# Attention with a shared bias on one core: the emission order from a list scheduler that models the queues, q/k transposes in halves, bias blocks four to a slot, first loads in quarters

## The chip, the cores and the metric

The kernel runs on one core of one Trainium2 chip. The metric is the device time of one execution in microseconds; lower is better. Times quoted at a place ("at 13.03") are counted from the start of the profiled span. In the views, PE is TensorE (PEld its weight load), ACT is ScalarE, DVE is VectorE, POOL is GpSimd, and SP only issues transfers here.

## What is computed

Softmax attention with one additive bias that all batches and heads share. There are 4 x 8 = 32 heads, 1024 queries and keys, and a head dimension of 64:

```python
batch, n_heads, seq_len, head_dim = 4, 8, 1024, 64
scores = (1.0 / np.sqrt(head_dim)) * np.matmul(q, k.transpose(0, 1, 3, 2))
scores = scores + bias                      # bias: (1, 1, 1024, 1024)
scores_max = np.max(scores, axis=-1, keepdims=True)
attn = np.exp(scores - scores_max) / (np.sum(np.exp(scores - scores_max), axis=-1, keepdims=True) + 1e-8)
return np.matmul(attn, v)
```

The kernel leaves the maximum out and uses exp(s + b) = exp(s) x exp(b). The row sums come out of the last matmul, because a column of ones stands behind v.

## The kernel before

**Units of work.** Two heads form a pair, so there are 16 pairs. q and k of a pair are transposed on PE (`L90`) into `px`. DVE copies k out as `kT`, with both heads stacked on the 128 partitions (`L101`), and q as `qT`, once for each head with the other head's half masked to zero (`L96`). A *bank* is a block of scores of 128 keys by 512 queries of one head: one matmul of 128x512 (`L126`) into one of three PSUM banks of a tile `ps`. There are 512 banks, 32 in a pair (2 halves of the queries, 8 key chunks, 2 heads).

**A slot** is one tile `ps`: up to three banks are filled on PE and taken by one exponential on ACT, which writes `E` in bf16 (`L128`). Two `ps` tiles alternate, so that the fill of one slot waits until ACT has emptied the slot two before it. The bias goes through the same two tiles: blocks of it are transposed on PE into `pb` (`L134`), and ACT takes the exponential into `eb` (`L138`). The bias is thus transformed once, in six slots of 3, 3 and 2 blocks for each half of the queries.

**Behind ACT.** DVE multiplies two banks of `E` at a time by `eb` (`L143`, 256 times). Then PE multiplies each bank by v: four matmuls of 128x65 (`L155`), which sum over the eight key chunks in a tile `po`. A finished `po` (one head, half of the queries) is divided by its row sums on DVE (`rs` in `L165`, `oall` in `L166`), and SP writes out each head.

**PSUM banks.** Six of the eight belong to the two `ps` tiles. The other two are called `xa` and `xb`. `po` of the pair's first head always takes `xa` and that of the second head `xb`. `px`, from the third pair on, always takes `xa`: 16 transposes of q, or 16 of k, at once.

**What sets the order.** Every engine runs its instructions in the order of the program, which is written out by hand under a manual schedule. A loop goes over the slots. After each slot's fill and exponential it emits up to three or four banks of the product with v (those whose multiplication was emitted at least `LAG = 3` steps ago), then one multiplication, the divisions that are due, and two more multiplications. A transposition is emitted at fixed counts of the products with v:

```python
pend_t += [(pr, 0, (pr - 2) * 32 + 8), (pr, 1, (pr - 2) * 32 + 24)]
```

**Start.** The first halves of k and q of pair 0 come as fp32 in one transfer each on SP and ACT (`k0f`, `q0f`), are cast, transposed and copied by the function `first`; all other loads go through POOL's queue. Eight matmuls on zeros (`wm`) run on PE while the first loads are under way. Slot 0 holds one bank, all others three, the last one.

Of the kernel before, what the change touches and what calls it, by code (L numbers as in the profile page):

```python
# [15 lines left out]
def kernel(  # L16
# [44 lines left out]
    mask = consts.tile([P, 2, S], BF)  # L61
# [3 lines left out]
    q0f = consts.tile([P, 2, QC, D], F32)  # L65
# [16 lines left out]
    def transpose(pr, which):  # L82
        transpose_pe(pr, which)()

    def transpose_pe(pr, which):
        src = raws[pr][which]
        px = ps_x.tile([P, NCH, P], BF, tag="xb" if pr < 2 and which else "xa", name="px")
        for c in range(NCH):
            for t in range(2):
                nc.tensor.transpose(px[t * D:(t + 1) * D, c, :], src[:, t, c, :], ident[:])  # L90

        def copy():
            if which == 0:

                dst = kvp.tile([P, 2, NCH * P], BF, name="qT")
                nc.vector.tensor_tensor(  # L96
                    dst[:], px.rearrange("p c q -> p (c q)").unsqueeze(1).to_broadcast([P, 2, NCH * P]),
                    mask[:], op=ALU.mult)
            else:
                dst = kvp.tile([P, NCH, P], BF, name="kT")  # L100
                nc.vector.tensor_copy(dst[:], px[:])  # L101
            trs[(pr, which)] = dst
        return copy
# [4 lines left out]
    slots = [list(range(1))] + [list(range(i, min(i + 3, NB))) for i in range(1, NB, 3)]  # L108
# [4 lines left out]
    def e_at(b, n):  # L113
        b = b + 2
# [4 lines left out]
    def s_slot(g):  # L119
        ps = ps_s.tile([P, 3, HQ], F32, tag="s", name="ps")  # L120
        sl = slots[g]
        n = len(sl)
        for j, b in enumerate(sl):
            pr, h, qh, kc = banks[b]
            qT, kT = trs[(pr, 0)], trs[(pr, 1)]
            nc.tensor.matmul(ps[:, j, :], kT[:, kc, :], qT[:, h, qh * HQ:(qh + 1) * HQ],  # L126
                             start=True, stop=True)
        nc.scalar.activation(e_at(sl[0], n), ps[:, :n, :], ACTF.Exp, scale=scale)  # L128

    def b_slot(qh, kcs):  # L130
        ps = ps_s.tile([P, 3, 2 * HQ], BF, tag="s", name="pb")
        for j, kc in enumerate(kcs):
            for i in range(QC):
                nc.tensor.transpose(ps[:, j, i * P:(i + 1) * P],  # L134
                                    btraw[:, qh * QC + i, :].rearrange("p (kp kc) -> p kc kp", kc=NCH)[:, kc, :],
                                    ident[:])
        n = len(kcs)
        nc.scalar.activation(eb[:, qh, kcs[0]:kcs[0] + n, :], ps[:, :n, :HQ], ACTF.Exp)  # L138

    def mul_pair(b, n=2):  # L140
        pr, h, qh, kc = banks[b]
        e = e_at(b, n)
        nc.vector.tensor_tensor(e, e, eb[:, qh, kc:kc + 1, :].to_broadcast([P, n, HQ]), op=ALU.mult)  # L143
# [4 lines left out]
    def av_bank(b):  # L148
# [23 lines left out]

    av_order = []
    for u in range(0, NB, 16):
        av_order += [u + 2 * i for i in range(8)] + [u + 2 * i + 1 for i in range(8)]

    with tc.manual_schedule():

        nc.sync.dma_start(out=k0f.rearrange("p t c d -> p t (c d)"), in_=kf[0][:, :, :QC * D])
        nc.scalar.dma_start(out=q0f.rearrange("p t c d -> p t (c d)"), in_=qf[0][:, :, :QC * D])  # L180
# [6 lines left out]
        raws[0] = (qr0, kr0)  # L187
        nc.gpsimd.dma_start(out=kr0[:, :, QC:, :].rearrange("p t c d -> p t (c d)"), in_=kf[0][:, :, QC * D:])
        nc.gpsimd.dma_start(out=qr0[:, :, QC:, :].rearrange("p t c d -> p t (c d)"), in_=qf[0][:, :, QC * D:])
        nc.gpsimd.dma_start(out=btraw[:, :QC, :], in_=bf_[:, :QC, :])  # L190
        for t in range(2):
            for u in range(2):
                nc.vector.memset(mask[t * D:(t + 1) * D, u, :], 1.0 if t == u else 0.0)  # L193
# [11 lines left out]
        nc.scalar.copy(kr0[:, :, :QC, :], k0f[:])  # L205
        nc.vector.tensor_copy(qr0[:, :, :QC, :], q0f[:])  # L206
        kT0 = kvp.tile([P, NCH, P], BF, name="kT")
        qT0 = kvp.tile([P, 2, NCH * P], BF, name="qT")
        trs[(0, 0)], trs[(0, 1)] = qT0, kT0
        def first(half):  # L210
            cs = slice(half * QC, (half + 1) * QC)
            pk = ps_x.tile([P, QC, P], BF, tag="xb", name="pk")
            pq = ps_x.tile([P, QC, P], BF, tag="xa", name="pq")
            for px, which in ((pk, 1), (pq, 0)):
                for c in range(QC):
                    for t in range(2):
                        nc.tensor.transpose(px[t * D:(t + 1) * D, c, :], raws[0][which][:, t, half * QC + c, :], ident[:])  # L217
            if half == 0:
                nc.scalar.copy(kT0[:, cs, :], pk[:])
            else:  # L220
                nc.vector.tensor_copy(kT0[:, cs, :], pk[:])  # L221
            qs = slice(half * HQ, (half + 1) * HQ)
            nc.vector.tensor_tensor(qT0[:, :, qs],  # L223
                                    pq.rearrange("p c q -> p (c q)").unsqueeze(1).to_broadcast([P, 2, HQ]),
                                    mask[:, :, qs], op=ALU.mult)
        first(0)
        s_slot(0)

        order = [("S", g) for g in range(1, NS)]
        halves = [(0, 1, 2), (3, 4, 5), (6, 7)]  # L230
        for at, x in ((5, (0, halves[0])), (7, (0, halves[1])), (9, (0, halves[2])),
                      (11, (1, halves[0])), (13, (1, halves[1])), (15, (1, halves[2]))):
            order.insert(at, ("B",) + x)

        mul_done = {}
        eb_have = set()
        mul_next = 0
        exp_b = 1
        av_next = 0

        pend_t = []
        for pr in range(2, NP):
            pend_t += [(pr, 0, (pr - 2) * 32 + 8), (pr, 1, (pr - 2) * 32 + 24)]
        LAG = 3

        def muls(n):
            nonlocal mul_next
            while n and mul_next < NB:
                pr, h, qh, kc = banks[mul_next]
                w = 2  # L250
                if mul_next + w > exp_b or (qh, kc) not in eb_have:
                    break
                mul_pair(mul_next, w)
                for b in range(mul_next, mul_next + w):
                    mul_done[b] = step
                mul_next += w
                n -= 1

        t_wait = None
        for step, item in enumerate(order):  # L260
            if item[0] == "S":
                g = item[1]
                s_slot(g)
                new_b = slots[g][-1] + 1
            else:
                b_slot(item[1], item[2])
                new_b = exp_b
            late = []
            if step == 1:
                first(1)  # L270
            if step == 8:
                transpose(1, 1)
                transpose(1, 0)
                load_qk(3)
            quota = 4 if (exp_b - av_next) > 18 else 3
            if t_wait is not None and step >= t_wait:
                pr, which, _ = pend_t.pop(0)
                late.append(transpose_pe(pr, which))
                t_wait = None
                quota = 1  # L280
                if which == 1:
                    if pr + 2 < NP:
                        load_qk(pr + 2)
                    load_v(pr)
            while quota and av_next < NB:
                b = av_order[av_next]
                if mul_done.get(b, 10 ** 9) > step - LAG:
                    break
                e = av_bank(b)
                if e:  # L290
                    late.append(e)
                av_next += 1
                quota -= 1
                if pend_t and av_next == pend_t[0][2]:
                    t_wait = step + 2

            muls(1)
            for f in late:
                f()
            muls(2)  # L300
            exp_b = new_b
            if item[0] == "B":
                for kc in item[2]:
                    eb_have.add((item[1], kc))

        while av_next < NB:
            muls(1)
            b = av_order[av_next]
            while mul_next <= b:
                muls(1)  # L310
            e = av_bank(b)
            if e:
                e()
            av_next += 1
# [30 lines left out]
```

## Time and profile before

| | us |
|---|---|
| median of 3 runs | 262.85 (262.81 to 264.83) |
| the profiled execution | 265.01 |
| its span in the trace | 263.1 |
| busy: ACT, DVE, PE | 242.0, 227.2, 220.6 |

The granted TensorE clock was 0.998 over the span. The span leaves out some 1.9 us that the profiled execution's own time holds around it. An engine's busy time counts the overlap of two of its instructions once. In a timeline a row merges equal instructions that follow each other: its start, how long it lasts in all, and in brackets the idle time ahead of it with what ended it.

### The profile page before, as it was taken

Reading aid. Unit: us, or ns where it says so; the run is one execution under the profiler, and the core shown is the slowest. Engines: PE = TensorE matmul, PEld = TensorE weight load, DVE = VectorE, ACT = ScalarE, POOL = GpSimd, SP = SyncE. Lnnn points to the kernel's source line nnn. Section 1 sums busy time; section 2 is a strip of 40 time slices with the busy share of each in tenths; the row PEclk is TensorE's granted clock in tenths of the full one; section 3 lists DMA queues with packets and bytes.
Section 4 is the critical chain, followed back from the end, with each engine's and each line's share of the span. In section 5 each row is a group of like instructions: output and inputs, shape, how many; then the busy total and the mean of one; then the engine's idle time right before and its main releaser. Section 6 shows DMA issues by size and latency. Waiting matters only on the chain.

```text
span 263.1 us, 7177 instructions
## 1 busy us (share of the span) xinstructions
PE 220.6 (84%) x3092; PEld 138.6 (53%) x3144; DVE 227.2 (86%) x425; ACT 242.0 (92%) x182; POOL 52.7 (20%) x72
## 2 busy tenths in 40 slices
PE   7857889888889888898988888888988889898882
PEld 2335655555555555555555555555655555555552
DVE  5218889999899999989989989998999999899893
ACT  4598999999999999999999999999999999999990
POOL 5834004040220404040030404022180000000000
PEclk9999999999999999999999999999999999999999
DMA  7999907759190856729191855819199202011112
GB/s 140 181 217 187 157 0 123 82 97 104 44 159 25 139 40 123 83 67 135 42 156 38 135 36 103 101 45 156 44 160 83 80 2 80 5 40 42 40 44 80
DMA packets 47455, 23.79 MB, mean 90 GB/s; under 512 B 34368, under 2 KB 43072, under 8 KB 47168
## 3 DMA queue, kind: packets, MB, share of 16 engines
q0 software_dynamic: 42272, 14.42, 51.1%
q1 hardware_dynamic: 4880, 8.65, 9.1%
q8 instruction: 24, 0.39, 0.6%
q10 hardware_dynamic: 272, 0.26, 0.4%
q14 instruction: 7, 0.06, 0.1%
HBM read 29.36 MB, written 8.39 MB: 143 GB/s over the span
## 4 chain that ended last, share of the span: by engine, by line
DVE 32%; PE 32%; ACT 31%; issue 3%; ACTq 0%; DVEq 0%
ACT E L128 30%; PE ps L126 21%; DVE E L143 18%; PE po L155 9%; DVE qT L96 6%; DVE kT L101 4%; DVE oall L166 2%; ACT eb L138 2%; DVE mask L193 1%; PE pq L217 1%; DVE rs L165 1%; ACTq L128 0%; DVE qT L223 0%; DVE qr L206 0%; PE px L90 0%
## 5 line engine op out<-in xcount | busy, mean ns | idle before, releaser
L128 ACT ACTIVATE E<-ps 128x1536 bf16<-128x1536 f32 (+1 forms) x172 | 232.7, 1470 | 10.6 <-PE ps L126 7.2
L143 DVE TENSOR_TENSOR E<-E,eb 128x1024 bf16<-128x1024 bf16 x256 | 166.9, 687 | 21.9 <-ACT E L128 11.1
L126 PE MATMUL ps<-qT,kT 128*128 128x512 bf16 x460 | 135.4, 383 | 15.8 <-ACT E L128 10.6
L155 PEld LDWEIGHTS <-E 128*128 128x128 bf16 x2048 | 84.0, 98 | 56.2 <-issue 21.2
L155 PE MATMUL po<-vall,E 128*128 128x65 bf16 x2048 | 93.6, 194 | 17.8 <-DVE qT L96 12.3
L126 PEld LDWEIGHTS <-kT 128*128 128x128 bf16 x512 | 44.4, 98 | 43.6 <-issue 19.1
L74 POOL DMA_DIRECT2D kr<-in_k_dram x15 | 10.5, 702 | 139.9 <-PE px L90 80.8
L166 DVE TENSOR_TENSOR oall<-po,rs 128x256 f32<-128x256 f32 x64 | 27.2, 425 | 2.2
L80 POOL DMA_DIRECT2D vall<-in_v_dram x32 | 28.1, 884 | 2.5 <-DVE qr L206 2.5
L96 DVE TENSOR_TENSOR qT<-px,mask 128x2048 bf16<-128x2048 bf16 x15 | 18.3, 1218 | 0.0
L165 DVE RECIPROCAL rs<-po 128x4 f32<-128x4 f32 x64 | 11.3, 176 | 0.7 <-PE po L155 0.7
L101 DVE COPY kT<-px 128x1024 bf16<-128x1024 bf16 x15 | 10.3, 684 | 0.9 <-PE px L90 0.9
L75 POOL DMA_DIRECT2D qr<-in_q_dram x15 | 10.8, 723 | 0.7 <-DMA vall<-in_v_dram 0.4
L90 PEld LDWEIGHTS <-kr 128*64 128x64 bf16 x240 | 7.1, 109 | 6.4 <-issue 6.4
L90 PE MATMUL px<-ident,qr 128*64 128x128 bf16 x240 | 9.5, 222 | 0.7
L90 PEld LDWEIGHTS <-qr 128*64 128x64 bf16 x240 | 7.2, 109 | 5.6 <-issue 3.4
L90 PE MATMUL px<-ident,kr 128*64 128x128 bf16 x240 | 9.6, 222 | 0.6
L138 ACT ACTIVATE eb<-pb 128x1536 bf16<-128x1536 bf16 (+1 forms) x6 | 8.0, 1332 | 0.0
L134 PEld LDWEIGHTS <-btraw 128*128 128x128 bf16 x64 | 4.8, 147 | 3.2 <-issue 2.5
L134 PE MATMUL pb<-ident,btraw 128*128 128x128 bf16 x64 | 5.0, 226 | 1.8 <-ACT eb L138 1.2
L203 PE MATMUL wm<-zeros 128*128 128x512 bf16 x8 | 3.6, 631 | 1.2 <-DVE zeros L182 1.2
L221 DVE COPY kT<-pk 128x512 bf16<-128x512 bf16 x1 | 0.4, 424 | 3.8 <-PE pk L217 3.8
(25 smaller groups left out, 17.0 us busy)
## 6 DMA issues: line engine op xcount, KB each, us to landing
out_dram<-oall SPq DMA_DIRECT2D x32, 256.0 KB, 2.2
vall<-in_v_dram POOLq DMA_DIRECT2D x32, 128.0 KB, 6.7
kr<-in_k_dram POOLq DMA_DIRECT2D x15, 256.0 KB, 4.0
qr<-in_q_dram POOLq DMA_DIRECT2D x15, 256.0 KB, 5.6
btraw<-in_bias_dram POOLq DMA_DIRECT2D x2, 1024.0 KB, 10.7
q0f<-in_q_dram ACTq DMA_DIRECT2D x1, 256.0 KB, 4.2
k0f<-in_k_dram SPq DMA_DIRECT2D x1, 256.0 KB, 3.7
kr<-in_k_dram POOLq DMA_DIRECT2D x1, 128.0 KB, 4.2
```

Source lines behind the costliest of these rows:

```text
L75: nc.gpsimd.dma_start(out=qr.rearrange("p t c d -> p t (c d)"), in_=qf[pr])
L80: nc.gpsimd.dma_start(out=vall[:, 2 * pr + t, :, :D], in_=vf[pr, :, t])
L90: nc.tensor.transpose(px[t * D:(t + 1) * D, c, :], src[:, t, c, :], ident[:])
L96: nc.vector.tensor_tensor(dst[:], px.rearrange("p c q -> p (c q)").unsqueeze(1).to_broadcast([P, 2, NCH * P]), mask[:], op=ALU.mult)
L101: nc.vector.tensor_copy(dst[:], px[:])
L126: nc.tensor.matmul(ps[:, j, :], kT[:, kc, :], qT[:, h, qh * HQ:(qh + 1) * HQ], start=True, stop=True)
L128: nc.scalar.activation(e_at(sl[0], n), ps[:, :n, :], ACTF.Exp, scale=scale)
L138: nc.scalar.activation(eb[:, qh, kcs[0]:kcs[0] + n, :], ps[:, :n, :HQ], ACTF.Exp)
L143: nc.vector.tensor_tensor(e, e, eb[:, qh, kc:kc + 1, :].to_broadcast([P, n, HQ]), op=ALU.mult)
L155: nc.tensor.matmul(acc[:, i, :], e[:, 0, i * P:(i + 1) * P], vall[:, 2 * pr + h, kc, :], start=(kc == 0 and i == 0), stop=(kc == NCH - 1), ...
L165: nc.vector.reciprocal(rs[:], acc[:, :, D:D1])
L166: nc.vector.tensor_tensor(oall[:, qh * QC:(qh + 1) * QC, :], acc[:, :, :D], rs[:].to_broadcast([P, QC, D]), op=ALU.mult)
```

## The change

1. **Order.** The loop with its quotas and its lag is gone. The program now steps through a model of ACT, PE and DVE with a cost for each operation, and emits on PE and DVE what the model would start next. A fill goes first when it can start; another piece of PE work is put ahead of it only if it would end 100 ns before ACT is through with the slot in between, less the fill's cost.
2. **Transposes.** q and k of a pair are transposed in halves of 8 transposes, each copied by a DVE instruction of half the size. They take whichever of `xa` and `xb` is free, as do the `po` tiles.
3. **Bias.** Four blocks to a slot, so four slots instead of six.
4. **First loads.** k of pair 0 in two pieces on SP, q head by head on ACT and SP; each piece has a cast, transposes and a copy of its own. Slots begin with one and two banks; the last holds two. The masking of the first q halves is replaced by two memsets of zeros.
5. **Last unit.** The products with v of the last 16 banks alternate between the two heads.

The core of the diff:

```diff
-        px = ps_x.tile([P, NCH, P], BF, tag="xb" if pr < 2 and which else "xa", name="px")
-        for c in range(NCH):
+        px = ps_x.tile([P, QC, P], BF, tag=tag, name="px")
+        for c in range(QC):
             for t in range(2):
-                nc.tensor.transpose(px[t * D:(t + 1) * D, c, :], src[:, t, c, :], ident[:])
+                nc.tensor.transpose(px[t * D:(t + 1) * D, c, :], src[:, t, half * QC + c, :], ident[:])
...
-    slots = [list(range(1))] + [list(range(i, min(i + 3, NB))) for i in range(1, NB, 3)]
+    slots = [[0], [1, 2]] + [list(range(i, min(i + 3, NB))) for i in range(3, NB, 3)]
...
-        nc.scalar.activation(eb[:, qh, kcs[0]:kcs[0] + n, :], ps[:, :n, :HQ], ACTF.Exp)
+    def b_exp(qh, k0):
+        nc.scalar.activation(eb[:, qh, k0:k0 + 4, :], open_ps.pop(("B", qh, k0))[:, :4, :], ACTF.Exp)
...
-            po[h] = ps_x.tile([P, QC, D1], F32, tag="xa" if h == 0 else "xb", name="po")
+            po[h] = ps_x.tile([P, QC, D1], F32, tag=tag, name="po")
...
-        nc.sync.dma_start(out=k0f.rearrange("p t c d -> p t (c d)"), in_=kf[0][:, :, :QC * D])
-        nc.scalar.dma_start(out=q0f.rearrange("p t c d -> p t (c d)"), in_=qf[0][:, :, :QC * D])
+        nc.sync.dma_start(out=k0f[:, :, :2].rearrange("p t c d -> p t (c d)"), in_=kf[0][:, :, :2 * D])
+        nc.scalar.dma_start(out=q0f[0].rearrange("p c d -> p (c d)"), in_=qf[0][:, 0, :QC * D])
+        nc.sync.dma_start(out=q0f[1].rearrange("p c d -> p (c d)"), in_=qf[0][:, 1, :QC * D])
+        nc.sync.dma_start(out=k0f[:, :, 2:].rearrange("p t c d -> p t (c d)"), in_=kf[0][:, :, 2 * D:QC * D])
...
-        first(0)
-        s_slot(0)
...
+        def k_first(c0, cast, copy):
+            cs = slice(c0, c0 + 2)
+            cast(kr0[:, :, cs, :], k0f[:, :, cs, :])
+            px = ps_x.tile([P, 2, P], BF, tag="xb", name="px")
...
+            copy(kT0[:, cs, :], px[:])
...
+        k_first(0, nc.scalar.copy, nc.scalar.copy)
+        q_first(0, nc.vector.tensor_copy)
+        s_fill(0)
+        s_exp(0)
+        q_first(1, nc.vector.tensor_copy)
+        s_fill(1)
+        s_exp(1)
+        k_first(2, nc.vector.tensor_copy, nc.vector.tensor_copy)
...
+        EXP, EXP0, QK, AV, TP = 427, 45, 216, 170, 350
+        MUL, COPYQ, COPYK, EVAC, SEM = 600, 650, 420, 620, 80
...
+        for at, x in ((5, (0, 0)), (7, (0, 4)), (11, (1, 0)), (13, (1, 4))):
+            order.insert(at, ("B",) + x)
...
+            limit = 1e12
+            if f:
+                limit = max(f[0], act_end_of(i - 1) - f[1] - 100)
...
+            for c in (pe_piece(), pe_av()):
+                if c is None:
+                    continue
+                start = max(t_pe, c[0])
+                if start + c[1] > limit:
+                    continue
+                if best is None or start < best[0]:
+                    best = (start,) + c[1:]
...
+            return min(c, key=lambda x: (max(x[0], t_dve + 100), x[1]))
```

On DVE, in the middle of the run, the order before is the following (`E<-E,eb` is a multiplication of two banks, `qT<-px` and `kT<-px` are the copies out of the transposes, `rs` and `oall` a division):

```order
L143 TENSOR_TENSOR E<-E,eb 128x1024 x3
L96 TENSOR_TENSOR qT<-px,mask 128x2048
L143 TENSOR_TENSOR E<-E,eb 128x1024 x2
L165 RECIPROCAL rs<-po 128x4
L166 TENSOR_TENSOR oall<-po,rs 128x256
L143 TENSOR_TENSOR E<-E,eb 128x1024 x3
```

and now, at a like place:

```order
L148 TENSOR_TENSOR E<-E,eb 128x1024
L101 COPY kT<-px 128x512
L148 TENSOR_TENSOR E<-E,eb 128x1024
L97 TENSOR_TENSOR qT<-px,mask 128x2x512
L148 TENSOR_TENSOR E<-E,eb 128x1024 x2
L170 RECIPROCAL rs<-po 128x4
L171 TENSOR_TENSOR oall<-po,rs 128x256
```

The copies are half as large and spread among the multiplications: 31 of `qT` and 31 of `kT` in place of 17 and 16.

At the end of the program DVE did this before (the last row but four is the multiplication of banks 510 and 511, and two divisions follow it):

```order
L165 RECIPROCAL rs<-po 128x4
L166 TENSOR_TENSOR oall<-po,rs 128x256
L143 TENSOR_TENSOR E<-E,eb 128x1024
L165 RECIPROCAL rs<-po 128x4
L166 TENSOR_TENSOR oall<-po,rs 128x256
L165 RECIPROCAL rs<-po 128x4
L166 TENSOR_TENSOR oall<-po,rs 128x256
```

and does this now:

```order
L148 TENSOR_TENSOR E<-E,eb 128x1024 x2
L170 RECIPROCAL rs<-po 128x4
L171 TENSOR_TENSOR oall<-po,rs 128x256
L148 TENSOR_TENSOR E<-E,eb 128x1024 x5
L170 RECIPROCAL rs<-po 128x4
L171 TENSOR_TENSOR oall<-po,rs 128x256
L170 RECIPROCAL rs<-po 128x4
L171 TENSOR_TENSOR oall<-po,rs 128x256
```

The division of the `po` of the last unit but one now stands ahead of the last five multiplications; before, one multiplication stood between the last three divisions. On PE that `po` gets the last 20 of its 32 matmuls behind the last fill.

On ACT, the order at the start before is:

```order
L205 CAST kr<-k0f 128x2x256
L219 COPY kT<-pk 128x512
L128 ACTIVATE E<-ps 128x512
L128 ACTIVATE E<-ps 128x1536 x5
L138 ACTIVATE eb<-pb 128x1536
```

and now:

```order
L213 CAST kr<-k0f 128x2x128
L218 COPY kT<-px 128x256
L130 ACTIVATE E<-ps 128x512
L130 ACTIVATE E<-ps 128x1024
L130 ACTIVATE E<-ps 128x1536 x5
L143 ACTIVATE eb<-pb 128x2048
```

The first bias slot stands behind 18 banks instead of 16.

More of the change, by code (lines that the diff above doesn't have):

```diff
@@ L60 @@
     eb = consts.tile([P, 2, NCH, HQ], BF)
[L61 removed]
+    mask = consts.tile([P, 2, HQ], BF)
     vall = consts.tile([P, 2 * NP, NCH, D1], BF)
     k0f = consts.tile([P, 2, QC, D], F32)
[L65 removed]
+    q0f = [consts.tile([P, QC, D], F32, name=f"q0f{t}") for t in range(2)]
     zeros = consts.tile([P, HQ], BF)
@@ new lines @@
+        NO = len(order)
+        T0 = 9000.0
+        t_act, t_pe, t_dve = T0 + 900, T0, T0
+        filled = []
+        act_end = []
+        x_free = {"xa": T0, "xb": T0}
+        x_unit = {}
+        bias_at = [13500, 22000]
+        raw_at = {0: 7000, 1: 17500, 2: 27500}
+        pieces = [(0, 1, 1), (0, 0, 1)]
+        for pr in range(1, NP):
+            pieces += [(pr, 1, 0), (pr, 0, 0), (pr, 1, 1), (pr, 0, 1)]
+        piece_end = {(0, 1, 0): T0, (0, 0, 0): T0}
+        eb_at = {}
+        exp_at = {0: T0 + 400, 1: T0 + 900, 2: T0 + 900}
@@ new lines, with unit_of, cost_act @@
+        mul_at = {}
+        mul_next = 0
+        av_order = []
+        for u in range(0, NB, 16):
+            if u + 16 < NB:
+                av_order += [u + 2 * i for i in range(8)] + [u + 2 * i + 1 for i in range(8)]
+            else:
+                av_order += list(range(u, NB))
+        av_next = 0
+        def unit_of(b):
+            return banks[b][:3]
+        dve_q = []
+        def cost_act(i):
+            item = order[i]
+            return EXP0 + EXP * (len(slots[item[1]]) if item[0] == "S" else 4)
```

310 lines of the change are left out of this document (189 added, 121 removed).

## The prediction

> **What bounds the kernel now.** I read the busy times first, then the waits, then ACT's timeline, since ACT is the busiest engine.
>
> ```profile
> PE 220.6 (84%) x3092; PEld 138.6 (53%) x3144; DVE 227.2 (86%) x425; ACT 242.0 (92%) x182; POOL 52.7 (20%) x72
> ```
>
> Three engines stand above 84%. The end is therefore set by ACT's work plus the time ACT waits. Two views give both: the groups by shape and ACT's timeline.
>
> ```profile
> L128 ACT ACTIVATE E<-ps 128x1536 bf16<-128x1536 f32 x170 | 231.6, 1479 | 8.9 <-PE ps L126 5.5 <-ACT E L128 2.4 <-PE pq L217 0.8
> L128 ACT ACTIVATE E<-ps 128x512 bf16<-128x512 f32 x2 | 1.4, 708 | 1.7 <-PE ps L126 1.7
> L138 ACT ACTIVATE eb<-pb 128x1536 bf16<-128x1536 bf16 x4 | 5.9, 1469 | 0.0
> L138 ACT ACTIVATE eb<-pb 128x1024 bf16<-128x1024 bf16 x2 | 2.1, 1058 | 0.0
> L96 DVE TENSOR_TENSOR qT<-px,mask 128x2048 bf16<-128x2048 bf16 x15 | 18.3, 1218 | 0.0
> L101 DVE COPY kT<-px 128x1024 bf16<-128x1024 bf16 x15 | 10.3, 684 | 0.9 <-PE px L90 0.9
> L223 DVE TENSOR_TENSOR qT<-pq,mask 128x1024 bf16<-128x1024 bf16 x2 | 1.4, 692 | 0.7 <-PE pq L217 0.7
> L221 DVE COPY kT<-pk 128x512 bf16<-128x512 bf16 x1 | 0.4, 424 | 3.8 <-PE pk L217 3.8
> ```
>
> ```profile
> 8.10 0.60 ACT L128 ACTIVATE E<-ps 128x512 bf16<-128x512 f32 x1 [1.66 <-PE ps L126]
> ...
> 13.03 4.14 ACT L128 ACTIVATE E<-ps 128x1536 bf16<-128x1536 f32 x3 [0.85 <-PE pq L217]
> 17.04 1.47 ACT L138 ACTIVATE eb<-pb 128x1536 bf16<-128x1536 bf16 x1
> ...
> 22.40 1.05 ACT L138 ACTIVATE eb<-pb 128x1024 bf16<-128x1024 bf16 x1
> 24.40 1.45 ACT L128 ACTIVATE E<-ps 128x1536 bf16<-128x1536 f32 x1 [0.95 <-PE ps L126]
> ...
> 33.96 16.36 ACT L128 ACTIVATE E<-ps 128x1536 bf16<-128x1536 f32 x12 [0.39 <-PE ps L126]
> 50.81 14.88 ACT L128 ACTIVATE E<-ps 128x1536 bf16<-128x1536 f32 x11 [0.49 <-ACT E L128]
> ```
>
> A slot of three banks lasts 1.479 us, but the row at 50.81 holds eleven in 14.88, so they follow each other every (14.88 - 1.479) / 10 = 1.340 us: neighbours overlap by 0.139. With that pitch I count what ACT could have done in each stretch.
>
> - 13.03 to 33.96 (20.93 us): nine slots of three x 1.340 = 12.06, four bias slots x (1.469 - 0.139) = 5.32, two x (1.058 - 0.139) = 1.84; together 19.22. **Lost: 1.7.**
> - 33.96 to 256.36, where the last exponential ends (row at 239.57 below): the other 159 slots of three x 1.340, and 0.708 for the last bank, are 213.77 of 222.40 us. **Lost: 8.6.**
>
> The waits name the cause.
>
> ```profile
> PE po L155 <- DVE qT L96: 12.3, 15, 1.0
> DVE E L143 <- ACT E L128: 11.1, 32, 0.7
> ACT E L128 <- PE ps L126: 7.2, 12, 1.7
> PE po L155 <- DVE kT L101: 4.2, 14, 0.4
> ```
>
> PE stands still 29 times behind a copy out of a transposition. One of them, in order of time:
>
> ```profile
> 76.61 0.64 PE L90 MATMUL px<-ident,qr 128*64 128x128 bf16 x16
> 77.31 0.81 PE L126 MATMUL ps<-qT,kT 128*128 128x512 bf16 x2
> 77.80 1.22 DVE L96 TENSOR_TENSOR qT<-px,mask 128x2048 bf16<-128x2048 bf16 x1
> 79.07 0.41 PE L155 MATMUL po<-vall,E 128*128 128x65 bf16 x8 [0.70 <-DVE qT L96]
> 79.31 0.81 PE L126 MATMUL ps<-qT,kT 128*128 128x512 bf16 x3
> 80.16 15.01 ACT L128 ACTIVATE E<-ps 128x1536 bf16<-128x1536 f32 x11 [0.31 <-PE ps L126]
> ```
>
> The transposes fill `xa`, and the next `po` is tied to `xa`. Its matmul waits 0.70 us at the head of PE's queue, the fill behind it starts at 79.31, and ACT stands still until 80.16, 0.85 us after the fill began. So a fill must start 0.85 us before ACT runs dry.
>
> **The change, part by part.**
>
> *Transposes in halves, in a free bank.* Removed: the tie of `po` to the bank of `px`. In the new order the first eight transposes usually stand between two products of one unit, which go on in the other bank, so nothing behind them waits for the copy. Per slot PE now has a fill (three banks, 0.64 by the start of 77.31 to the end of issue at 77.95) and mostly four products (0.65) or two products and eight transposes (0.33 + 0.32): 1.29 or 1.30 of 1.340 us. By the order, only five of 176 slots hold more than 0.66 beside the fill, two of these beside the longer bias slots. The spare in the loop: ACT frees a slot 1.479 after its start, the fill follows 0.17 later (row at 254.57 below) and needs 0.85, 2.50 in all, against 2 x 1.340 = 2.68; 0.18 us is left. Bounds of what remains of the 8.6 us: nothing, if no fill is late by more than that; 4 us, if the 45 slots with transposes are each late by 0.09. I take 1.0, nearer to nothing, because the work of each slot fits. **Gain 7.6.** DVE pays for the halves: 31 x 0.692 against 18.3 + 1.4 is 1.8 us, and 31 x 0.424 against 10.3 + 0.4 is 2.4. These 4.2 us lie beside ACT as long as DVE's 227.2 + 4.2 stay below ACT's 242; without that cover they would be paid in full.
>
> *Order in the first 34 us.* The losses at 24.40 and 33.96 came the same way (16 to 32 transposes at once), and the new order holds at most 16 there. **Gain 1.7**; the bounds are 0 and 1.7.
>
> *Bias in four slots.* Four blocks: 1.469 + (1.469 - 1.058) - 0.139 = 1.741, four times 6.96, against 5.32 + 1.84 = 7.16. **Gain 0.2.** The first bias slot now stands behind 18 banks instead of 16, so DVE's first multiplication comes later by two banks less what the start gains; DVE then has nine multiplications waiting, which the 72 banks of `E` hold.
>
> *First loads in quarters.* Here PE matters.
>
> ```profile
> 1.23 3.59 PE L203 MATMUL wm<-zeros 128*128 128x512 bf16 x8 [1.23 <-DVE zeros L182]
> ...
> 5.37 0.64 DVE L206 CAST qr<-q0f 128x512 bf16<-128x512 f32 x1 [0.89 <-DMA q0f<-in_q_dram]
> ...
> 6.06 0.64 PE L217 MATMUL pq<-ident,qr 128*64 128x128 bf16 x8 [0.25 <-DVE qr L206]
> ...
> 6.74 0.69 DVE L223 TENSOR_TENSOR qT<-pq,mask 128x1024 bf16<-128x1024 bf16 x1 [0.73 <-PE pq L217]
> 7.48 3.15 PE L126 MATMUL ps<-qT,kT 128*128 128x512 bf16 x7 [0.78 <-DVE qT L223]
> ...
> 12.80 0.83 PE L126 MATMUL ps<-qT,kT 128*128 128x512 bf16 x3 [0.22 <-issue]
> ```
>
> These are estimates from the rows above. With q's first head alone, the cast starts at 4.6, as PE is at `wm` until 4.82 anyway, and takes 0.35, half of 0.64 and a little; four transposes take 0.45 against 0.68 for eight (6.06 to 6.74); the copy takes the 0.42 of `L221`; a fill of one bank, and 0.62 from it to ACT as before (7.48 to 8.10): the first exponential at 6.5, **1.6 earlier**. But then the next pieces come one behind the other. The second head of q is transposed after that fill (6.3), copied by 7.2, slot 1 is filled until 8.1 and ACT takes it at 8.3. The rest of k follows: transposes 8.1, copy until 8.9, slot 2 filled until 10.2 at 0.43 a bank, the speed of the row at 7.48. Sixteen transposes stand ahead of slot 3 (until 11.4), which ACT takes at 12.3 to 12.9, with six banks behind it. Before, it had done seven at 13.03; the seventh takes 0.45 more, so 12.75 to 13.35 against 13.03. **Nothing, +-0.3**; with early landings or a slow PE, 0.9 gained to 1.0 lost.
>
> *The end.* Which division stands ahead of which multiplication decides here.
>
> ```profile
> 239.57 16.79 ACT L128 ACTIVATE E<-ps 128x1536 bf16<-128x1536 f32 x13
> ...
> 250.34 1.28 DVE L143 TENSOR_TENSOR E<-E,eb 128x1024 bf16<-128x1024 bf16 x2
> ...
> 254.57 0.38 PE L126 MATMUL ps<-qT,kT 128*128 128x512 bf16 x1 [0.17 <-ACT E L128]
> ...
> 256.50 0.18 DVE L165 RECIPROCAL rs<-po 128x4 f32<-128x4 f32 x1
> ...
> 257.06 0.68 DVE L143 TENSOR_TENSOR E<-E,eb 128x1024 bf16<-128x1024 bf16 x1
> 257.79 1.16 PEld L155 LDWEIGHTS <-E 128*128 128x128 bf16 x36 [0.97 <-DVE E L143]
> ...
> 258.13 0.18 DVE L165 RECIPROCAL rs<-po 128x4 f32<-128x4 f32 x1 [0.39 <-PE po L155]
> ...
> 259.33 0.42 DVE L166 TENSOR_TENSOR oall<-po,rs 128x256 f32<-128x256 f32 x1
> ```
>
> Let T be the end of the last exponential, 256.36 before. The last `oall` ended at 259.75, T + 3.39. Now the last slot holds two banks (1.09, between 0.708 and 1.479), the slot before it starts at T - 2.43, and the one that the last fill waits for ends at T - 3.77 + 1.48 = T - 2.29. The fill starts 0.17 later and takes 0.43; the 20 matmuls behind it take 5 x 0.163 and end at T - 0.88. The division of that `po` starts 0.34 after its last four matmuls began (257.79 to 258.13), at T - 0.70, and holds DVE for 0.56 (256.50 to 257.06). Only then come five multiplications, 0.60 apart (1.28 for two of 0.68): the last ends at T + 2.94. Its products, 0.05 + 0.34, and two divisions (0.56, then 0.64) end at **T + 4.53: 1.1 lost**. At best the division finds its `po` early, which gives 1.0 gained; at worst another 0.5 is lost.
>
> **Sum.** -7.6 - 1.7 - 0.2 + 0 + 1.1 = -8.4 us. The profiled execution took 265.01 with a span of 263.1, and stands 2.2 above the median of 262.85; the sum is made against its span, 263.1 - 8.4 = 254.7, and taken off the median: **254.4 us**.
>
> **The rivals.**
>
> *A slow PE at the start.* At 7.48 the fills go at 0.43 us a bank (3.15 for seven), at 12.80 at 0.21. If the holes between the small pieces keep PE at the slow rate until slot 8, three banks take 1.28, the loop is 1.479 + 0.17 + 1.28 + 0.2 = 3.13 for two slots, 1.56 instead of 1.34, some 1.1 us for five slots: 255.5, within the range. The Trainium skill, "TensorE: Matmul & The Clock Gate", What's actually happening, says that the array's clock is held at half until a window of some 3.4 us is busy. By that rule the trace agrees: the fast rate comes about 3.4 us after the unbroken work from 7.48 on. Chance 0.2, and it leaves the sign.
>
> *Part of the stalls stays.* The slots with transposes overrun their 0.18 us, and half of 8.6 is left: 254.4 + 3.3 = 257.7. For it speaks how small the spare is; against it, that PE's work per slot fits. Chance 0.13.
>
> *The change doesn't do what it says.* If a `po` still finds its bank held by `px` at each change of unit, the 16.5 us of PE's waits above stay, ACT's 10.3 come back, and the end costs 1.1 more: 254.4 + 9.3 = 263.7, no change. Against it speaks the new order. Chance 0.08.
>
> *DVE becomes the bound.* There are now 58 pieces of transposes after the first pair's, each a wait for PE at the head of DVE's queue, with multiplications behind it for which PE's products wait. Each costs ACT only what goes beyond the 0.18 us. From 0.18 + 8.4 / 58 = 0.32 us a piece on, the gain is gone; at 0.40 the loss is 58 x 0.22 = 12.8, so 267.2: slower. For it speaks DVE's 86% before and 4.2 us more; against it, that DVE waited 11.1 us for ACT's exponentials before. Chance 0.06.
>
> **How the numbers follow.** My forecast has 0.53, the slow start 0.2, the half stalls 0.13, no change 0.08, slower 0.06. Low: 254.4 less the 1.0 left of stalls, less 0.9 at the start and 1.0 of the end, 251.5. High: the half stalls with some slow start, 259. A measurement of this kernel tells about 1% (2.6 us) from no change; so faster 0.86, same 0.08, slower 0.06.
>
> **What would show it.** ACT's timeline after some 30 us should be one run without idle time; waits of `po` for `qT` and `kT` should fall from 16.5 us to below 3. The first exponential should start near 6.5 and slot 3 between 12.3 and 12.9. The last `oall` should end 4.5 us after the last exponential. I am wrong if ACT waits for `ps` all along, if slot 3 starts after 14, or if PE waits for multiplications in every pair.

## The result and the profile after

The changed kernel takes 254.06 us (median of 4 executions, 253.68 to 256.28) against 263.3 before: ratio 0.966, 95% interval 0.959 to 0.973. On another chip it took 253.68 against 264.05: 0.960, 0.958 to 0.963. The forecast was 254.4. Its profiled execution took 254.24, with a span of 252.5 against 263.1.

The busy times first, then two rows of its waits (who waits for whom, us in all, times, longest):

```profile
PE 229.4 (91%) x3090; PEld 141.6 (56%) x3144; DVE 226.3 (90%) x461; ACT 239.1 (95%) x180; POOL 52.6 (21%) x72
```

```profile
ACT E L130 <- PE ps L125: 2.1, 3, 0.9
...
PE po L160 <- DVE oall L171: 0.8, 1, 0.8
```

ACT waits 2.1 us for fills instead of 7.2, and the 16.5 us in which products waited for `qT` and `kT` have no row any more. ACT's timeline:

```profile
6.20 0.60 ACT L130 ACTIVATE E<-ps 128x512 bf16<-128x512 f32 x1 [0.92 <-PE ps L125]
7.65 1.02 ACT L130 ACTIVATE E<-ps 128x1024 bf16<-128x1024 f32 x1 [0.85 <-PE ps L125]
8.96 6.82 ACT L130 ACTIVATE E<-ps 128x1536 bf16<-128x1536 f32 x5 [0.28 <-PE ps L125]
...
19.45 1.88 ACT L143 ACTIVATE eb<-pb 128x2048 bf16<-128x2048 bf16 x1 [0.56 <-PE pb L138]
...
30.14 214.61 ACT L130 ACTIVATE E<-ps 128x1536 bf16<-128x1536 f32 x160
```

160 exponentials stand in one row without idle time. Behind the last one, which ends at T = 30.14 + 214.61 = 244.75, the timeline of PE and DVE reads:

```profile
242.53 0.59 PE L125 MATMUL ps<-qT,kT 128*128 128x512 bf16 x2
...
242.97 0.90 PE L160 MATMUL po<-vall,E 128*128 128x65 bf16 x24
...
243.92 0.18 DVE L170 RECIPROCAL rs<-po 128x4 f32<-128x4 f32 x1
...
244.47 3.09 DVE L148 TENSOR_TENSOR E<-E,eb 128x1024 bf16<-128x1024 bf16 x5
...
247.96 0.18 DVE L170 RECIPROCAL rs<-po 128x4 f32<-128x4 f32 x1 [0.39 <-PE po L160]
...
248.72 0.42 DVE L171 TENSOR_TENSOR oall<-po,rs 128x256 f32<-128x256 f32 x1
```

The division at 243.92 waited for products behind the last fill, five multiplications follow it, and the last `oall` ends at 249.14, T + 4.39. The two profiled executions differ by 10.6 us, stretch by stretch:

| stretch | before | after | difference | forecast |
|---|---|---|---|---|
| seven banks done | 13.03 | 8.96 + 1.34 + 0.45 = 10.75 | -2.3 | 0 |
| ACT's loss up to the long run | 1.7 | 0.8 | -0.9 | -1.7 |
| bias, four slots | 7.16 | 4 x (1.881 - 0.139) = 6.97 | -0.2 | -0.2 |
| ACT's loss in the long run | 8.6 | 0.5 (159 x 1.340 + 1.02 of 214.61) | -8.1 | -7.6 |
| last exponential to last `oall` | 3.39 | 4.39 | +1.0 | +1.1 |
| sum | | | -10.5 | -8.4 |

So three of the five terms were right in size, and the start and the order up to the long run were not. Whether their causes were right, the experiments had to say. Times are compared with the kernel before on the same chip in the same job; the intervals are of 95%.

### The profile page after: what moved, and what is told of

It reads as the page before. It is cut to its first block, busy times and chain, and to the rows that moved or that the text cites. A ratio compares the mean times of both kernels' runs of the same rounds, so it can differ in the third digit from the quotient of the medians.

```text
span 252.5 us, 7217 instructions
## 1 busy us (share of the span) xinstructions
PE 229.4 (91%) x3090; PEld 141.6 (56%) x3144; DVE 226.3 (90%) x461; ACT 239.1 (95%) x180; POOL 52.6 (21%) x72
## 4 chain that ended last, share of the span: by engine, by line
PE 44%; ACT 35%; DVE 10%; DMA 4%; issue 3%; POOL 1%; ACTq 1%
ACT E L130 33%; PE ps L125 30%; PE po L160 8%; DVE E L148 6%; PE px L88 6%; DMA qr<-in_q_dram 4%; ACT eb L143 2%; DVE oall L171 1%; DVE qT L97 1%; POOL vall L80 1%; DVE mask L199 1%; DVE rs L170 1%; ACTq L130 1%; PE pb L138 0%; POOL kr L74 0%
## 5 line engine op out<-in xcount | busy, mean ns | idle before, releaser
L130 ACT ACTIVATE E<-ps 128x1536 bf16<-128x1536 f32 (+2 forms) x172 | 230.1, 1668 | 2.1 <-PE ps L125 2.1
L148 DVE TENSOR_TENSOR E<-E,eb 128x1024 bf16<-128x1024 bf16 x256 | 163.5, 683 | 1.0 <-ACT eb L143 1.0
L125 PE MATMUL ps<-qT,kT 128*128 128x512 bf16 x458 | 134.5, 378 | 12.9 <-ACT E L130 4.7
L160 PE MATMUL po<-vall,E 128*128 128x65 bf16 x2048 | 96.4, 194 | 2.4 <-DVE E L148 1.0
L74 POOL DMA_DIRECT2D kr<-in_k_dram x15 | 10.5, 699 | 96.4 <-PE px L88 91.5
L97 DVE TENSOR_TENSOR qT<-px,mask 128x1024 bf16<-128x1024 bf16 x31 | 21.3, 688 | 2.3 <-PE px L88 1.6
L101 DVE COPY kT<-px 128x512 bf16<-128x512 bf16 x31 | 13.1, 424 | 10.5 <-PE px L88 9.7
L170 DVE RECIPROCAL rs<-po 128x4 f32<-128x4 f32 x64 | 11.4, 179 | 3.1 <-PE po L160 2.7
L88 PE MATMUL px<-ident,qr 128*64 128x128 bf16 x248 | 12.8, 224 | 1.0 <-DMA qr<-in_q_dram 0.9
L88 PE MATMUL px<-ident,kr 128*64 128x128 bf16 x248 | 12.8, 225 | 0.2
L143 ACT ACTIVATE eb<-pb 128x2048 bf16<-128x2048 bf16 x4 | 7.5, 1881 | 0.6 <-PE pb L138 0.6
L209 PEld LDWEIGHTS <-zeros 128*128 128x128 bf16 x8 | 1.0, 142 | 2.9 <-issue 1.6
```

The costliest lines, as they stand in the source:

```text
L88: nc.tensor.transpose(px[t * D:(t + 1) * D, c, :], src[:, t, half * QC + c, :], ident[:])
L97: nc.vector.tensor_tensor(dst[:, :, half * HQ:(half + 1) * HQ], px.rearrange("p c q -> p (c q)").unsqueeze(1).to_broadcast([P, 2, HQ]), ma ...
L101: nc.vector.tensor_copy(dst[:, half * QC:(half + 1) * QC, :], px[:])
L130: nc.scalar.activation(e_at(slots[g][0], n), open_ps.pop(("S", g))[:, :n, :], ACTF.Exp, scale=scale)
L143: nc.scalar.activation(eb[:, qh, k0:k0 + 4, :], open_ps.pop(("B", qh, k0))[:, :4, :], ACTF.Exp)
L160: nc.tensor.matmul(acc[:, i, :], e[:, 0, i * P:(i + 1) * P], vall[:, 2 * pr + h, kc, :], start=(kc == 0 and i == 0), stop=(kc == NCH - 1), ...
```

## Experiments on the start

**The changed kernel again**, for a second trace of its start.

> The changed kernel once more, for a second look at its start. In the first profile ACT had seven banks done at 10.75 us (slot 2 starts at 8.96, slot 3 follows 1.34 later, a bank takes 0.45), against 13.03 before, and a fill went at 0.21 us a bank from 7.02 on. Theory 'clock': the fast rate of PE at 7 us was this execution's luck; in another one it can be slow (0.43 us a bank) until 10 or 12 us, and then slot 3 starts at 12.3 to 12.9 as predicted. Theory 'pieces': the small pieces are what makes the start early, and slot 3 starts at 10.3 again, with the time within 1 us of 254.

253.68 us, 0.960 (0.958 to 0.963). The start was the same, and the bias slot at 19.45 did not wait this time:

```profile
8.97 6.82 ACT L130 ACTIVATE E<-ps 128x1536 bf16<-128x1536 f32 x5 [0.29 <-PE ps L125]
...
29.52 214.61 ACT L130 ACTIVATE E<-ps 128x1536 bf16<-128x1536 f32 x160
```

**The old start in the changed kernel.**

```diff
+        nc.sync.dma_start(out=k0f.rearrange("p t c d -> p t (c d)"), in_=kf[0][:, :, :QC * D])
+        nc.scalar.dma_start(out=q0f.rearrange("p t c d -> p t (c d)"), in_=qf[0][:, :, :QC * D])
...
-        k_first(0, nc.scalar.copy, nc.scalar.copy)
-        q_first(0, nc.vector.tensor_copy)
...
+        s_fill(0)
+        s_exp(0)
+        s_fill(1)
+        s_exp(1)
```

> The changed kernel with the first loads of before: one transfer each for the first halves of k and q, a cast, eight transposes and a copy for each; slots, order model and all else as changed. Theory 'pieces': the first exponential is back at 8.1 and seven banks are done 1.5 to 2.3 us later than in the changed kernel, so 255.5 to 256.3. Theory 'clock': with PE at its fast rate the fills behind the first copy take 0.21 us a bank, ACT runs through from 8.0 on, and seven banks are done at 11.2 to 11.3, 0.5 us later: 254.5; with PE slow (0.43 a bank) at about 13.1, 2.3 later.

254.49 us, 0.964 (0.960 to 0.968), four executions from 253.84 to 256.11; the interval overlaps that of the changed kernel. The profiled one was the slowest, and its PE was slow: six fills in 2.72 us. Slot 3 starts at 12.58 and a bank takes 0.45, so seven banks are done at 13.03, as theory 'clock' had it for a slow PE (13.1).

```profile
7.44 2.72 PE L125 MATMUL ps<-qT,kT 128*128 128x512 bf16 x6 [0.79 <-DVE qT L217]
...
12.58 5.48 ACT L130 ACTIVATE E<-ps 128x1536 bf16<-128x1536 f32 x4 [0.94 <-PE ps L125]
```

**No matmuls on zeros.** The eight `wm` are left out.

```diff
-        for i in range(8):
-            nc.tensor.matmul(wm[:, i % 3, :], zeros[:, :P], zeros[:], start=True, stop=True)
```

> The changed kernel without the eight matmuls on zeros ahead of the first transposes, so that PE idles until k's first piece has landed. Theory 'clock': PE is slow (0.43 us a bank) through the first slots, slot 3 starts at 12 to 13 instead of 10.3, and the whole is 1.5 to 2.5 us slower, 255.5 to 256.5. Theory 'pieces': the rate of PE matters little, because the copies on DVE and ACT set the pace of the start; under 0.5 us slower.

255.88 us, 0.968 (0.966 to 0.970): some 2.2 us slower than the changed kernel on the same chip, as theory 'clock' had it, with all four executions between 255.55 and 256.15. In its trace slot 2 is filled at 0.43 us a bank, and slot 3 starts at 12.58, where the prediction had put it (12.3 to 12.9):

```profile
8.97 1.50 PE L125 MATMUL ps<-qT,kT 128*128 128x512 bf16 x3
...
12.58 5.48 ACT L130 ACTIVATE E<-ps 128x1536 bf16<-128x1536 f32 x4 [0.62 <-PE ps L125]
```

**The new start in the kernel before.** The start is as in the changed kernel; the mask stays at its old full size, since the whole copies need it.

```diff
+    slots = [[0], [1, 2]] + [list(range(i, min(i + 3, NB))) for i in range(3, NB, 3)]
...
+        k_first(0, nc.scalar.copy, nc.scalar.copy)
+        q_first(0, nc.vector.tensor_copy)
+        s_slot(0)
+        q_first(1, nc.vector.tensor_copy)
+        s_slot(1)
+        k_first(2, nc.vector.tensor_copy, nc.vector.tensor_copy)
```

> The kernel before with the start of the changed one alone (loads in quarters, slots of one and two banks first, two banks last); loop, lag, banks and bias as before. Theory 'pieces': 1.5 to 2.3 us faster than before, 261.0 to 261.8. Theory 'clock': within 0.5 us of before where both have PE at the same rate. Either way the waits of the products for qT and kT stay at 16.5 us.

266.25 us, 1.008 (1.005 to 1.010): 2.2 us slower, which neither theory had. The products' waits for `qT` and `kT` stayed, as both had it (12.3 and 4.3 us). The memsets of the full mask and the new ones of `qT` keep DVE until the cast at 5.91 instead of 4.32, and PE waits 1.3 us for it. PE is also slow in its fills (whether because of the wait, no run shows), and slot 3 starts at 14.12:

```profile
5.91 0.49 DVE L220 CAST qr<-q0f 128x256 bf16<-128x256 f32 x1 [0.88 <-issue]
...
14.12 5.48 ACT L127 ACTIVATE E<-ps 128x1536 bf16<-128x1536 f32 x4 [0.57 <-PE ps L125]
```

**What follows for the start.** The start has two speeds, and the loads in quarters are not what tells them apart. In the pair of traces of the result, PE was slow before (seven fills in 3.15 us at 7.48) and fast after (two in 0.59, from 7.02). A kernel of the next section has the old start with a fast PE:

```profile
7.26 1.87 PE L126 MATMUL ps<-qT,kT 128*128 128x512 bf16 x7 [0.79 <-DVE qT L223]
```

```profile
7.67 7.47 ACT L128 ACTIVATE E<-ps 128x512 bf16<-128x512 f32 x6 [1.65 <-PE ps L126]
...
30.36 215.53 ACT L128 ACTIVATE E<-ps 128x1536 bf16<-128x1536 f32 x161
```

Its first six slots stand without a gap from 7.67, so seven banks are done at 7.67 + 7.47 - 1.48 - 2 x 1.34 = 10.98 (the row's end, less the last slot and two pitches). The changed kernel has them at 10.75. The quarters thus bring 0.2 us when PE is fast, and some 2.1 of the 2.3 us in the table are the rate. When PE is slow they lose 0.4: a trace of the last section of experiments has the new start with a slow PE and slot 3 at 12.99, thus seven banks at 13.44, against 13.03 with the old start.

## Experiments on the middle of the run

**Whole transposes, in any free bank.** Only the first pair keeps its halves.

```diff
-            pieces += [(pr, 1, 0), (pr, 0, 0), (pr, 1, 1), (pr, 0, 1)]
+            pieces += [(pr, 1, None), (pr, 0, None)]
...
+                if half is None:
+                    cost = 620 if which else 1160
```

> The changed kernel with q and k of pairs 1 to 15 transposed whole again, 16 transposes and one copy each (the first pair stays in halves), still in any free bank and placed by the order model, which is given 700 ns for the transposes and 620 and 1160 for the copies. Theory 'the tie of banks': halves are not needed, the stalls stay gone, and ACT's run after 30 us has no idle time; 253.7 +-0.7, or a little less, as DVE's copies cost 4 us less and its order now leaves four multiplications behind the last but two divisions. Theory 'halves': 16 transposes beside a fill overrun the 0.18 us that the loop spares, a slot loses 0.1 to 0.3, 30 times: 256.7 to 262.

251.95 us, 0.955 (0.952 to 0.958), and 251.99 when run again on another chip: **faster than the changed kernel**. The two were not timed on one chip, and their intervals just meet, but the traces show where the 1.7 us come from. ACT's long run is as tight as with halves. At the end three multiplications are left instead of five: T is 29.76 + 214.61 = 244.37, and the last `oall` ends at 246.96, T + 2.59.

```profile
29.76 214.61 ACT L138 ACTIVATE E<-ps 128x1536 bf16<-128x1536 f32 x160
...
243.48 1.90 DVE L156 TENSOR_TENSOR E<-E,eb 128x1024 bf16<-128x1024 bf16 x3 [0.24 <-ACT E L138]
...
246.54 0.42 DVE L179 TENSOR_TENSOR oall<-po,rs 128x256 f32<-128x256 f32 x1
```

**Whole transposes, and the banks tied as before.** Of the change's part in the middle only the order is left.

```diff
-            tags = sorted((x_free[x], x) for x in x_free if x != busy)
+            tags = [(x_free["xa"], "xa")] if busy != "xa" else []
...
-                free, tag = min((x_free[x], x) for x in x_free)
+                tag = "xa" if banks[b][1] == 0 else "xb"
+                free = x_free[tag]
```

> The same with the banks tied as before: whole transposes always in xa, po of the first head in xa, of the second in xb; only the order model is left of the change in the middle of the run. Theory 'the tie of banks': with the tie back the products wait for the copies again, and most of the 8 us return: 259 to 262. Theory 'the order': the model knows of the tie and puts the transposes early in the second head's products, so that the copy is done when xa is wanted; 253.7 to 255.

252.05 us, 0.958 (0.952 to 0.963). The free bank is not needed either. Its timeline around a transposition shows why:

```profile
88.12 0.42 DVE L179 TENSOR_TENSOR oall<-po,rs 128x256 f32<-128x256 f32 x1
...
89.72 0.64 PE L90 MATMUL px<-ident,kr 128*64 128x128 bf16 x16
...
90.33 0.81 PE L133 MATMUL ps<-qT,kT 128*128 128x512 bf16 x3
...
90.40 0.69 DVE L102 COPY kT<-px 128x1024 bf16<-128x1024 bf16 x1
...
90.97 0.65 PE L168 MATMUL po<-vall,E 128*128 128x65 bf16 x16
```

The copy starts as soon as the transposes end (90.36), and a fill lies between them and the next products. In the trace before, the copy at 77.80 began 0.55 us after its transposes had ended (76.61 + 0.64), behind a multiplication.

**The kernel before, its transposes one step earlier.**

```diff
-                    t_wait = step + 2
+                    t_wait = step + 1
```

> The kernel before with one number changed: the transposition is emitted one step after its count is reached instead of two (t_wait = step + 1), so one slot earlier in the same order, with whole transposes in the tied bank. Theory 'the order': the copy gets 1.34 us more before the first head's po wants xa, the waits for qT and kT fall from 16.5 us to below 4, and ACT gains 5 to 8 us: 256 to 259. Theory 'the tie of banks': the transposes now wait for the division that empties xa, PE stands still there instead, and the time stays within 2 us of 264.

266.93 us, 1.011 (1.006 to 1.016): slower. The rival's wait came true: the products' waits for the copies fall from 16.5 us to 0.8, but the transposes wait for the division that empties `xa`, 28 times. ACT's loss in the long run rises from 8.6 to 11.4 us (160 x 1.340 + 0.71 of 226.49). One of the waits:

```profile
PE px L90 <- DVE oall L166: 15.7, 28, 0.6
```

```profile
88.35 0.69 DVE L143 TENSOR_TENSOR E<-E,eb 128x1024 bf16<-128x1024 bf16 x1 [0.65 <-ACT E L128]
...
88.96 0.17 DVE L165 RECIPROCAL rs<-po 128x4 f32<-128x4 f32 x1
...
89.17 0.42 DVE L166 TENSOR_TENSOR oall<-po,rs 128x256 f32<-128x256 f32 x1
...
89.75 0.64 PE L90 MATMUL px<-ident,qr 128*64 128x128 bf16 x16 [0.56 <-DVE oall L166]
```

The division itself stands behind a multiplication, which waited 0.65 us for ACT.

**The kernel before, with the divisions and copies ahead of the step's first multiplication, and t_wait = step + 1.**

```diff
-            muls(1)
             for f in late:
                 f()
-            muls(2)
+            muls(3)
...
-                    t_wait = step + 2
+                    t_wait = step + 1
```

> The kernel before with two things of its order changed: the transposition one step after its count (t_wait = step + 1), and on DVE the divisions and copies that are due ahead of the first multiplication of the step instead of behind it. Tied banks, whole transposes, six bias slots and the old start stay. Theory 'the place in the order is all': with the division 0.6 us earlier the transposes no longer wait for it (15.7 us, 28 times, with t_wait alone), nor the products for the copies; ACT's run after 34 us loses under 3 us instead of 8.6, and the time is 257 to 259. Rival: DVE, held by divisions and copies that wait for PE, falls behind with its multiplications, the products wait for these, and the time stays at 262 or more.

254.73 us, 0.966 (0.963 to 0.970). **Two small edits to the order written by hand come within about 1 us of the whole change**, with tied banks, whole transposes, six bias slots and the old start. ACT's run from 30.36 on, shown above, has no idle time; it loses 0.4 us, where under 3 were expected. The time lies 2.3 us below the 257 to 259 of the expectation; in the trace PE was fast at the start, which is worth 2.1 against the trace before (10.98 instead of 13.03).

**DVE's order alone, of these two edits**: the divisions and copies go ahead, and the transposition stays at step + 2.

> The kernel before with the second of the two edits alone: divisions and copies ahead of the step's first multiplication on DVE, the transposition at its old place (t_wait = step + 2). With the first edit alone 266.9, with both 254.7. Theory 'DVE's order': a copy no longer stands behind a multiplication (0.6 us), so the products' waits for qT and kT fall from 16.5 us to some 5, the loss after 34 us from 8.6 to 2 to 4 us, and the time is 257 to 260. Theory 'both are needed': with 8 of 32 matmuls left when the transposes come, the copy is late whatever stands ahead of it, and the time is 262 or more.

257.18 us, 0.975 (0.971 to 0.979). The waits of the products for `qT` fall from 12.3 to 5.7 us and those for `kT` vanish; what is left hardly reaches ACT, whose long run loses 1.45 us (159 x 1.340 + 0.71 of 215.22) instead of 8.6:

```profile
PE po L155 <- DVE qT L96: 5.7, 15, 0.8
```

```profile
33.99 215.22 ACT L128 ACTIVATE E<-ps 128x1536 bf16<-128x1536 f32 x160 [0.39 <-PE ps L126]
```

The profiled execution (257.73) has the same slow start as the one before (slots at 8.11, 9.39 and 13.05), so the two can be laid side by side: the same 160 exponentials take 215.22 instead of 222.40 us. **DVE's order alone brings 7.2 us in the old kernel, of the 8.1 of the main term.** The transposition one step earlier adds 1.0 in the long run (a loss of 0.42 instead of 1.45); beside that, the two traces differ by 2.1 us at the start, where PE was fast in one and slow in the other.

## Experiments on the end and on PE's rate

**Costs as the trace shows them**, in the changed kernel's order model.

```diff
-        EXP, EXP0, QK, AV, TP = 427, 45, 216, 170, 350
-        MUL, COPYQ, COPYK, EVAC, SEM = 600, 650, 420, 620, 80
+        EXP, EXP0, QK, AV, TP = 427, 59, 214, 163, 325
+        MUL, COPYQ, COPYK, EVAC, SEM = 602, 600, 340, 550, 80
```

> The changed kernel with the costs of its order model set to what the trace shows: a slot of three 1340 ns, a multiplication 602, the half copies 600 and 340, a division 550, a fill's bank 214, a product 163, eight transposes 325. With them DVE's work for a pair (13.7 us) is below ACT's (14.3); with the costs as changed it is above (14.2 against 14.1). Theory 'DVE lags in the model only': the products follow the exponentials more closely, the division of the last unit but one no longer waits for 20 matmuls behind the last fill, and the last oall ends some 2.4 us after the last exponential instead of 4.4: 251.7. Rival: DVE is really short of time at the end, and the tail stays at 4 us or more: 253.5.

255.21 us, 0.968 (0.965 to 0.971), no faster; but the end is as expected:

```profile
10.60 1.45 ACT L130 ACTIVATE E<-ps 128x1536 bf16<-128x1536 f32 x1 [0.76 <-PE ps L125]
12.99 5.48 ACT L130 ACTIVATE E<-ps 128x1536 bf16<-128x1536 f32 x4 [0.94 <-PE ps L125]
...
32.46 215.08 ACT L130 ACTIVATE E<-ps 128x1536 bf16<-128x1536 f32 x160
```

```profile
246.66 1.90 DVE L148 TENSOR_TENSOR E<-E,eb 128x1024 bf16<-128x1024 bf16 x3 [0.24 <-ACT E L130]
...
249.71 0.43 DVE L171 TENSOR_TENSOR oall<-po,rs 128x256 f32<-128x256 f32 x1
```

T is 32.46 + 215.08 = 247.54, and the last `oall` ends at 250.14, T + 2.60 instead of 4.39. The start took 2.9 us more (32.46 against 29.52), because PE was slow, with the same code at the start as the changed kernel. The other three executions have no trace, but all four times lie within 0.01 us of each other. So the late end is the order model's doing: its costs make DVE the bound, and it lets the multiplications trail. ACT's long run takes 0.5 us more here (215.08 against 214.61); no run shows why.

**Two matmuls on zeros more**, in the kernel with whole transposes, and that kernel again beside it.

```diff
+        for _ in range(pad):
+            nc.tensor.matmul(ps[:, 2, :], zeros[:, :P], zeros[:], start=True, stop=True)
...
-        s_fill(0)
+        s_fill(0, pad=1)
...
-        s_fill(1)
+        s_fill(1, pad=1)
```

> The kernel with whole transposes (e4), and two more matmuls on zeros at the start: one ahead of slot 0's fill and one ahead of slot 1's, into a bank that the slot doesn't use, where PE stands still for the copy of q. Theory 'the rate of PE at the start depends on whether it was busy': PE comes to its fast rate by some 8 us in every execution, slot 3 starts before 11, no execution takes the 2 us more that single ones did, and the times lie within 0.5 us of 251.9. Rival, that the rate is luck and nothing in the program moves it: one execution in four or so still takes 254; or the matmuls are in the way of the fills and all take 0.3 us more.

> The kernel with whole transposes as it was, on the same chip as the one with the two matmuls more. Under 'busy' and under 'luck' alike most executions take 251.8 to 252.1 and one or two of six 253.8 to 254.2, with slot 3 at 12.6 to 13 in these instead of 10.6.

251.95 us (251.85 to 252.49) and 251.99 (251.75 to 252.13). No time in either lies near 254, where a slow PE would put it, although one or two of six were expected there without the two matmuls. So the pair says nothing on whether they help. They do no harm.

## Why the prediction was right, and where it was not

- *What bounds the kernel*: right. ACT's work plus its waits gave the place and the size: 8.6 and 1.7 us lost, of which 8.1 and 0.9 came back.
- *Transposes in halves, in a free bank*: the size was right (7.6 forecast, 8.1 measured), the cause wrong. The step that failed reads "Removed: the tie of `po` to the bank of `px`". Whole transposes in tied banks run as tight (252.05). What the old order lost by is the multiplication of 0.6 us ahead of copies and divisions on DVE: swapping these alone gives 7.2 us. The quoted rows had shown it: the copy at 77.80 began 0.55 us late, and PE waited 0.70 us. In the changed kernel the copies do come sooner: between 34 and 240 us they begin 0.11 us after the end of their transposes on average, against 0.56 before. But with whole transposes in tied banks it is 0.24 and no product waits for a copy either, since other work lies between. How much each of the two does in the changed kernel is open: it was not run with DVE's old order.
- *DVE's cost of the halves*, which "lie beside ACT": right in the long run, which stands without idle time. The kernel without the halves is 1.7 us faster at the end, but the halves as such do not stretch it: with the model's costs corrected they end at T + 2.60, as whole transposes do (T + 2.59). What stretched the end is how the model, given its costs, ordered the work.
- *Order in the first 34 us*: -1.7 forecast, -0.9 measured. In the second trace of the changed kernel the bias slot did not wait, and the long run began at 29.52, 0.6 us earlier, which makes the term -1.5.
- *Bias*: right, 0.2.
- *First loads in quarters*: "nothing, +-0.3" nearly held at equal rates of PE (0.2 gained when it is fast, 0.4 lost when it is slow). In the pair of traces the term was -2.3, because PE was fast in one and slow in the other. The rival of a slow PE at the start was worth 2.2 us, not 1.1, and the execution that it describes is the one without `wm`. Its reading that the fast rate comes "about 3.4 us after the unbroken work from 7.48 on" is off, although that work goes on without a hole: transposes and fills are still slow at 10.98 and 11.55, and the trace's clock record has the full clock from 12.84 on, 5.4 us after 7.48.

```profile
10.98 0.63 PE L217 MATMUL pq<-ident,qr 128*64 128x128 bf16 x8
11.55 1.03 PE L126 MATMUL ps<-qT,kT 128*128 128x512 bf16 x2
```

- *The end*: +1.1 forecast, +1.0 measured, by the steps named: division, five multiplications, products, two divisions.
- *The rivals* "part of the stalls stays", "doesn't do what it says" and "DVE becomes the bound" did not occur: ACT's long run has no gap, with DVE busy for 90% of the span. (The last of them counts 58 pieces of transposes; the 31 and 31 copies less the two of the first pair are 60, which changes little.)
- That the sum came out within 0.4 us of the median is partly luck. Without the start, the terms of the pair of traces add up to -8.2 (forecast: -8.4), because the long run gave 0.5 more and the order 0.8 less. The start, forecast at nothing, was -2.3 in that pair: the profiled execution before had the slow PE and stood 2.2 above its median. The sum was taken off the median, which left this out.

## What to carry to other kernels

Where an engine's queue holds both bulk work and the short operations that give a buffer back, put the short ones first: one multiplication of 0.6 us ahead of copies and divisions cost 7 us of 264. Before a scheduler, halves or free buffers are credited with a gain, try the smallest edit of the old order that removes the same wait. And look at the end on its own: there the work that trails the bounding engine is no longer hidden.

## What the runs showed of the hardware

PE's rate at the start is not fixed by the program. At the start each trace goes once from the slow rate (0.43 us a bank) to the fast one (0.21), and its clock record has the moment from which the full clock is granted. (The mean clock of a page, such as 0.998, counts the time before that record as full, so it does not show a slow start.) The same code, the start of the kernel before, turns at 12.84 and 13.00 in two traces and at 5.13 and 5.14 in two others. The start of the changed kernel turns between 4.31 and 6.21 in six traces (one of them with the two matmuls more), and at 13.99 in the one with the model's other costs; without `wm` it turns at 12.09. The old start in the changed kernel turns at 12.51, the new start in the kernel before at 13.58. No turn lies between 6.21 and 12.09. The late one cost 2 to 3 us where two such traces can be compared. How long `wm` takes does not tell the two apart: 3.59 or 3.60 us in both kinds, and 3.40 and 3.45 where the turn comes before its end. What decides is not shown.

Only one execution of each run has a trace. By their times, the start was fast in all four executions of the changed kernel's second job, slow in all four with the model's other costs, and slow in all four without `wm`.

The Trainium skill, "TensorE: Matmul & The Clock Gate", What's actually happening, says that the window in which PE must be busy runs free of the kernel's start. By that rule the early turns agree: they come 3.1 to 5.0 us after PE's first matmul, at no fixed distance. Why the late ones come only 11.3 to 12.8 us after it, with `wm` in place, no run here shows.
